# Placing prepared weight tiles at eight byte offsets inside longer rooms, in an order that changes from group to group

## The chip, the cores and the metric

The kernel runs on one core of one Trainium2 chip. The metric is the device time of one execution in microseconds (us). Three runs of the kernel before took 1741.55, 1745.67 and 1746.55 us; their median, 1745.67 us, is the time before.

## The reference: what is computed

One layer of a diffusion backbone over 256 latent and 256 context tokens of width 2048, all in float32: a bidirectional gated linear recurrence (HGRN2, 16 heads of 128) as token mixer, then a gated MLP with a width-3 depthwise convolution. Each sub-layer has a norm before and after it and shift, scale and gate from a linear map of SiLU(c). Only the latent stream is returned. Cut to the core, for the one layer there is:

```python
h_l = modulate(rms_norm(x, norm_mix_pre), sh_ml, sc_ml)          # and h_c from ctx
y_l, _ = hgrn2_mixer(h_l, h_c, hgrn_w_in, lower_bounds, hgrn_o_norm, hgrn_w_out, False)
x = x + gt_ml * rms_norm(y_l, norm_mix_post)
h_l = modulate(rms_norm(x, norm_ffn_pre), sh_fl, sc_fl)
gate, up = jnp.split(h_l @ ffn_w_in, 2, axis=-1)
f_l = (jax.nn.silu(dwconv_centred(gate, conv_w, conv_b)) * up) @ ffn_w_out
return x + gt_fl * rms_norm(f_l, norm_ffn_post)
```

In the mixer `h @ hgrn_w_in` gives q, two forget gates (f, b), v and an output gate g, each of width 2048; the recurrence runs over chunks in both directions, and its normed and gated output goes through `hgrn_w_out`.

## The kernel before, in words

**Three matmuls for one.** Every large product is made by `mm3` (L195 to L199). Each float32 operand is split into a high part, rounded to the matmul's input type, and a low part, the rest. `mm3` adds three products into one bank: high by high (L197), high by low (L198), low by high (L199). In each, `lhsT` is the stationary operand, loaded ahead of the matmul by its own weight load, and `rhs` is the moving operand, streamed through the array.

**The weight stream.** `Stream` (L108) walks all 456 weight tiles of the program in a fixed list: 40 tiles of 2 x 512 columns for the start, 120 of 4 x 256 for the six later head pairs, 32 for `w_out`, 176 for `ffn_w_in` and 88 for `ffn_w_out`. Each holds 1024 float32 values in each of the 128 partitions, 4096 bytes. `load` (L118) brings it into one of four `w_raw` buffers with one DMA on SyncE's queue; `prep` (L125) splits it with `split` (L103): ScalarE casts it to `w_hi` (L105), VectorE writes the rest to `w_lo` (L106). There are three `w_hi` and three `w_lo` buffers (rooms) in `wpool`, and two more of each in `hold` for the last chunk of the mixer's output product. `next` (L144) hands out a tile and keeps two more prepared ahead, so a room is written again as soon as the matmuls of the tile that lay in it are done.

**The stages.** In the start (L347 on) the modulated tokens hTh and hTl come into being two k-tiles at a time, and each pair meets five weight tiles. Then, for each of six head pairs (L869), come the projections f and b (512 columns of hTh and hTl moving, weights stationary), q and g (`proj_ws`, 256 columns moving) and v (`proj_xs`: here the weights are moving, 256 columns, and hTh, hTl stationary). Between their tiles, `step` (L851) lets in pieces of the recurrence (`scan`, float32 matmuls and transposes of 128 columns or fewer) and of the gates' map (`ada_part`). `out_product` (L947) makes the mixer's output product: zh, zl stationary, 512 columns of weights moving. The FFN's first product (L1037 to L1057) has weights stationary and 256 columns of h2h, h2l moving, 4,224 matmuls; its second is `out_product` again with ah, al stationary and 512 columns of weights moving, 1,056 matmuls.

**Places in SBUF.** Tiles lie where their pools put them, one behind the other from the left or, with `side="right"`, from the right end. `spacer` (L57) makes a tile of given length that nobody uses. Four of these concern the change: `spacer(wpool, SHIFT)` (L518, 64 bytes) stands between the `w_raw` and the `w_hi` rooms, `spacer(h2, 256 - SHIFT)` (L933) ahead of h2h and h2l, `spacer(hold[0], SHIFT)` (L940) ahead of the rooms in `hold`; `SHIFT` is 64 (L63). With them, every `w_hi` and `w_lo` begins 64 bytes past a multiple of 128, and so does all that lies behind `wpool` on the left up to h2: keep, st, zpool, sp. hTh, hTl, zh, zl, h2h, h2l, ah and al begin at a multiple of 128. All inner steps (512, 1024 and 2048 bytes) are multiples of 128.

Of the kernel before, what the change touches and what calls it, by code (L numbers as in the profile page):

```python
# [9 lines left out]
F32R = mybir.dt.float32r  # L10
# [7 lines left out]
P = 128  # L18
# [17 lines left out]
def tile_hgrn2_convffn_layer(  # L36
# [13 lines left out]
    wpool = ctx.enter_context(tc.tile_pool(name="wpool", bufs=3))  # L50
# [6 lines left out]
    def spacer(pool, nbytes):  # L57

        pool.tile([P, nbytes // 4], F32, name="spacer", bufs=1)

    SHIFT = 64  # L63
    edge = ctx.enter_context(tc.tile_pool(name="edge", bufs=1, side="right"))
    spacer(edge, 224)

    def bank(pool, name):
        return pool.tile([P, 512], F32, name=name)
# [34 lines left out]
    def split(hi, lo, src):  # L103

        S.copy(out=hi, in_=src)  # L105
        V.tensor_tensor(out=lo, in0=src, in1=hi.bitcast(F32), op=ALU.subtract)  # L106

    class Stream:  # L108


# [14 lines left out]
        def prep(self, pool=wpool):  # L125
            i = len(self.done)
            with tc.high_priority(offset=0 if i < n_start else 400):
                self.load(i + 1)
                _, a, w = self.specs[i]
                hi = pool.tile([P, a, w], F32R, name="w_hi")  # L130
                lo = pool.tile([P, a, w], F32R, name="w_lo")
                if i in self.fine:
                    for j in range(a):
                        split(hi[:, j], lo[:, j], self.raw[i][:, j])
                else:
                    split(hi, lo, self.raw[i])
            self.raw[i] = None
            self.done.append((hi, lo))
# [82 lines left out]
    def rows128(v):  # L221
        return v.rearrange("(r p) -> r p", p=P)
# [26 lines left out]
    def load_tokens(src, tiles):  # L249
        for tt in range(2):  # L250
            t = hpool.tile([P, D], F32, name=f"hTh{len(tiles)}")
            nc.sync.dma_start(out=t, in_=src[tt * P:(tt + 1) * P, :])
            tiles.append(t)
# [11 lines left out]
    def silu_c():  # L265

        tp = bank(ps_mi, "mi")
        PE.transpose(out=tp[:, 0:32], in_=rowsS[0:32, :], identity=ident[0:32, 0:32])
        sgc = st.tile([P, 32], F32, name="sgc")
        S.activation(out=sgc, in_=tp[:, 0:32], func=AF.Sigmoid)  # L270
        V.tensor_tensor(out=cst[:, :, 0:2], in0=tp[:, 0:32].rearrange("p (i k) -> p k i", i=2),
                        in1=sgc.rearrange("p (i k) -> p k i", i=2), op=ALU.mult)
# [6 lines left out]
    def column(dst, src, n):  # L279

        tp = bank(ps_sc, "sc")
        PE.transpose(out=tp[:, 0:n], in_=src[0:n, :], identity=ident[0:n, 0:n])
        V.tensor_copy(out=dst[:, 0:n], in_=tp[:, 0:n])
# [29 lines left out]
    def normed(w):  # L313

        for i in range(2):
            t = xt[2 * w + i]
            ms = small.tile([P, 1], F32, name="ms")
            jk = st.tile([P, D], F32, name="jk")
            S.activation(out=jk, in_=t, func=AF.Square, accum_out=ms)
            r = token_rstd(ms, "rstd")  # L320
            for cs in (slice(0, 256), slice(256, D)):
                V.tensor_scalar(out=t[:, cs], in0=t[:, cs], scalar1=r, scalar2=None, op0=ALU.mult)
# [66 lines left out]
    def ada_load(j2):  # L389
        aws = []  # L390
        for r4 in range(4):
            aw = st.tile([P, 4, 2, 256], F32, name="aw", bufs=4)
            for s in range(2):
                nc.sync.dma_start(
                    out=aw[:, :, s, :],
                    in_=ada_w[r4 * 512:(r4 + 1) * 512, s * D + j2 * 256:s * D + (j2 + 1) * 256].rearrange(
                        "(a p) n -> p a n", p=P))
            aws.append(aw)
        return aws
# [111 lines left out]
    with tc.manual_schedule():  # L511
        nc.sync.dma_start(out=rowsS[0:16], in_=rows128(c[0]))
        nc.sync.dma_start(out=rowsS[16:32], in_=rows128(c_ctx))
        load_tokens(x, xt)
        nc.sync.dma_start(out=rowsB[0:96], in_=rows128(ada_b))
        nc.sync.dma_start(out=rows0[0:16], in_=rows128(n_mix_pre[0]))
        ws.load(1)
        spacer(wpool, SHIFT)  # L518
        aws0 = ada_load(0)
        ws.load(4)  # L520
        V.memset(ones32, 1.0)
        V.memset(one1, 1.0)
        V.memset(eps1, EPS)
        nc.gpsimd.memset(cst, 0.0)
        make_identity(nc, ident)
        silu_c()
        normed(0)
        ws.prep()
        column(colsB, rowsB, 96)
        column(cols0, rows0, 16)  # L530
        strip = bank(ps_o, "o")
        ada_rows(strip, aws0, 0)
        turned(0, 0, KT)
        for r4 in range(1, 4):
            ada_rows(strip, aws0, r4)
        mod0 = ada_mod(0, strip)
        load_tokens(ctx_in, xt)
        for i in range(2):
            q4 = hpool.tile([P, 4, 512], F32R, name=f"hTh{i}")
            for k in range(4):  # L540
                hTh[4 * i + k] = q4[:, k]
        for k in range(2):
            hTl[k] = hpool.tile([P, 512], F32R, name=f"hTl{k}")
        modulated(0, mod0, (0,))
        ws.prep()
        ws.prep()
# [366 lines left out]
    h2h, h2l, xin, hold = [], [], [], []  # L913

    def mixed():

        nonlocal h2
        with tc.high_priority(offset=200):
            split(zh[1], zl[1], z[1])
        for p in (*range(2, NP - 1), 0):  # L920
            split(zh[p], zl[p], z[p])
            for _ in range(MIXSTEP):
                next(mix, None)
            yield
        for _ in mix:
            pass
        split(zh[NP - 1], zl[NP - 1], z[NP - 1])
        yield
        yield
        zp_ctx.close()  # L930
        sp_ctx.close()
        h2 = h_ctx.enter_context(tc.tile_pool(name="h2", bufs=1))
        spacer(h2, 256 - SHIFT)  # L933
        for k in range(KT // 2):
            h2h.append(h2.tile([P, 2, T], F32R, name=f"h2h{k}"))
            h2l.append(h2.tile([P, 2, T], F32R, name=f"h2l{k}"))

        xinp = xin_ctx.enter_context(tc.tile_pool(name="xinp", bufs=1))
        hold.append(xin_ctx.enter_context(tc.tile_pool(name="hold", bufs=MORE)))
        spacer(hold[0], SHIFT)  # L940
        for i in range(4):
            xin.append(xinp.tile([P, D // 2], F32, name=f"xin{i}"))
            nc.sync.dma_start(out=xin[i], in_=x[i // 2 * P:(i // 2 + 1) * P, i % 2 * 1024:(i % 2 + 1) * 1024])

    h2 = None
# [91 lines left out]
    for i in range(NFF):  # L1037
# [6 lines left out]
        for up in range(2):  # L1044
            o = bank(ps_pj, "pj")
            for k4 in range(4):
                hi, lo = ws.next()
# [70 lines left out]
```

## Time and profile before

| what | value |
|---|---|
| runs: lowest, median, highest | 1741.55, 1745.67, 1746.55 us |
| the profiled execution's own time | 1748.88 us |
| its span, first to last instruction | 1747.1 us |
| mean granted TensorE clock | 0.994 |
| instructions | 32106 |
| DMA | 352.57 MB, 202 GB/s in the mean |

The span is what the views below divide up; 1.8 us of the execution lie around it. "PE" is TensorE's matmul side and "PEld" its weight loads, which run beside the matmuls. A matmul's record begins when it begins and ends when its last result is out, so records of matmuls that follow each other closely overlap: how fast they follow is read from the distance of the starts, or from how many stand in a stretch, not from the recorded length. [...]

### The profile page before, as it was taken

Reading aid. Unit: us, or ns where it says so; the run is one execution under the profiler, and the core shown is the slowest. Engines: PE = TensorE matmul, PEld = TensorE weight load, DVE = VectorE, ACT = ScalarE, POOL = GpSimd, SP = SyncE. Lnnn points to the kernel's source line nnn. Section 1 sums busy time; section 2 is a strip of 40 time slices with the busy share of each in tenths; the row PEclk is TensorE's granted clock in tenths of the full one; section 3 lists DMA queues with packets and bytes.
Section 4 is the critical chain, followed back from the end, with each engine's and each line's share of the span. In section 5 each row is a group of like instructions: output and inputs, shape, how many; then the busy total and the mean of one; then the engine's idle time right before and its main releaser. Section 6 shows DMA issues by size and latency. Waiting matters only on the chain.

```text
span 1747.1 us, 32106 instructions
## 1 busy us (share of the span) xinstructions
PE 1689.7 (97%) x13022; PEld 1501.7 (86%) x13022; DVE 1159.0 (66%) x1877; ACT 777.5 (45%) x1197; POOL 3.4 (0%) x13
## 2 busy tenths in 40 slices
PE   6999999999999999999999799999999999999998
PEld 4677888888989889897987598999999999888886
DVE  5777897865649775786566788666666666544444
ACT  4322264454545344343464554444444444443443
POOL 0000000000000000000000000000000000000000
PEclk9999999999999999999999999999999999999999
DMA  9887656653326773776358688666666666655554
GB/s 349 283 290 243 215 171 205 214 164 105 103 84 201 248 241 103 231 226 196 110 176 293 206 262 276 199 194 194 193 194 193 193 194 194 205 199 193 199 191 146
DMA packets 274646, 352.57 MB, mean 202 GB/s; under 512 B 12954, under 2 KB 197675, under 8 KB 273987
## 3 DMA queue, kind: packets, MB, share of 16 engines
q1 hardware_dynamic: 274499, 350.53, 62.4%
q8 instruction: 102, 1.67, 0.4%
q14 instruction: 45, 0.37, 0.1%
HBM read 348.37 MB, written 2.11 MB: 201 GB/s over the span
## 4 chain that ended last, share of the span: by engine, by line
PE 74%; DMA 12%; DVE 9%; issue 3%; ACT 1%; SPq 1%; DVEq 0%; ACTq 0%
PE pj L197 23%; PE pj L198 23%; PE pj L199 23%; DMA ada_w<-in_ada_w_dram 10%; DVE w_lo L106 3%; DVE ada_acc L351 2%; PE o L403 1%; DMA w_raw<-in_hgrn_w_in_dram 1%; DVE k L679 1%; PE sc L719 1%; ACT w_hi L105 1%; PE mi L791 1%; DMA aw<-in_ada_w_dram 1%; DMA hTh<-in_x_dram 0%; DVE QA L679 0%
## 5 line engine op out<-in xcount | busy, mean ns | idle before, releaser
L106 DVE TENSOR_TENSOR w_lo<-w_raw,w_hi 128x1024 fp32r<-128x1024 f32 (+1 forms) x465 | 558.6, 1203 | 364.9 <-ACT w_hi L105 363.8
L105 ACT CAST w_hi<-w_raw 128x1024 fp32r<-128x1024 f32 (+1 forms) x465 | 478.5, 1032 | 704.8 <-PE pj L198 384.7
L199 PE MATMUL pj<-h2h,w_lo 128*128 128x256 f32 x1408 | 389.5, 277 | 4.8 <-DVE w_lo L106 4.7
L197 PE MATMUL pj<-h2h,w_hi 128*128 128x256 f32 x1408 | 389.2, 276 | 0.0
L198 PE MATMUL pj<-h2l,w_hi 128*128 128x256 f32 x1408 | 389.1, 276 | 0.0
L197 PE MATMUL pj<-hTh,w_hi 128*128 128x256 f32 (+1 forms) x1040 | 353.4, 341 | 2.9 <-ACT hTh L105 1.6
L199 PE MATMUL pj<-hTh,w_lo 128*128 128x256 f32 (+1 forms) x1040 | 348.4, 336 | 5.5 <-DVE w_lo L106 5.4
L198 PE MATMUL pj<-hTl,w_hi 128*128 128x256 f32 (+1 forms) x1040 | 348.2, 335 | 0.0
L199 PEld LDWEIGHTS pj<-h2h,w_lo 128*128 128x128 f32 x1408 | 264.3, 188 | 5.9 <-DVE w_lo L106 5.8
L197 PEld LDWEIGHTS pj<-h2h,w_hi 128*128 128x128 f32 x1408 | 264.4, 188 | 0.9 <-issue 0.8
L198 PEld LDWEIGHTS pj<-h2l,w_hi 128*128 128x128 f32 x1408 | 264.4, 188 | 0.2 <-DVE h2l L106 0.2
L351 DVE SCALAR_TENSOR_TENSOR ada_acc<-ada_w,cst,ada_acc 128x512 f32<-128x512 f32 x240 | 179.8, 749 | 82.4 <-DMA ada_w<-in_ada_w_dram 80.2
L197 PEld LDWEIGHTS pj<-hTh,w_hi 128*128 128x128 f32 x1040 | 196.7, 189 | 33.0 <-issue 5.9
L199 PEld LDWEIGHTS pj<-hTh,w_lo 128*128 128x128 f32 x1040 | 196.7, 189 | 28.9 <-DVE w_lo L106 6.3
L198 PEld LDWEIGHTS pj<-hTl,w_hi 128*128 128x128 f32 x1040 | 197.1, 190 | 21.4 <-DVE hTl L106 0.2
L199 PE MATMUL pj<-w_hi,al 128*128 128x512 f32 x352 | 138.7, 394 | 0.0
L198 PE MATMUL pj<-w_lo,ah 128*128 128x512 f32 x352 | 138.0, 392 | 0.0
L197 PE MATMUL pj<-w_hi,ah 128*128 128x512 f32 x352 | 136.6, 388 | 0.0
L197 PE MATMUL pj<-w_hi,hTh 128*128 128x256 f32 (+1 forms) x448 | 134.2, 299 | 1.7 <-DVE q L455 1.5
L198 PE MATMUL pj<-w_lo,hTh 128*128 128x256 f32 (+1 forms) x448 | 132.3, 295 | 0.0
L199 PE MATMUL pj<-w_hi,hTl 128*128 128x256 f32 (+1 forms) x448 | 132.2, 295 | 0.0
L197 PEld LDWEIGHTS pj<-w_hi,hTh 128*128 128x128 f32 x448 | 84.2, 188 | 6.5 <-ACT w_hi L105 1.6
(224 smaller groups left out, 1773.5 us busy)
## 6 DMA issues: line engine op xcount, KB each, us to landing
w_raw<-in_ffn_w_in_dram SPq DMA_DIRECT2D x176, 512.0 KB, 4.0
w_raw<-in_hgrn_w_in_dram SPq DMA_DIRECT2D x160, 512.0 KB, 4.5
ada_w<-in_ada_w_dram SPq DMA_DIRECT2D x256, 256.0 KB, 3.9
w_raw<-in_ffn_w_out_dram SPq DMA_DIRECT2D x88, 512.0 KB, 3.7
aw<-in_ada_w_dram SPq DMA_DIRECT2D x64, 512.0 KB, 8.7
w_raw<-in_hgrn_w_out_dram SPq DMA_DIRECT2D x32, 512.0 KB, 5.7
hTh<-in_x_dram SPq DMA_DIRECT2D x2, 1024.0 KB, 7.0
hTh<-in_ctx_dram SPq DMA_DIRECT2D x2, 1024.0 KB, 12.0
```

What stands on the lines that cost most here:

```text
L105: S.copy(out=hi, in_=src)
L106: V.tensor_tensor(out=lo, in0=src, in1=hi.bitcast(F32), op=ALU.subtract)
L197: PE.matmul(out=o, lhsT=lh, rhs=rh, start=first, stop=False, skip_group_check=True)
L198: PE.matmul(out=o, lhsT=lh, rhs=rl, start=False, stop=False, skip_group_check=True)
L199: PE.matmul(out=o, lhsT=ll, rhs=rh, start=False, stop=last, skip_group_check=True)
L351: V.scalar_tensor_tensor(out=acc, in0=aw, scalar=cst[:, r, 0:1], in1=acc, op0=ALU.mult, op1=ALU.add)
L403: PE.matmul(out=strip[32 * a:32 * (a + 1), :], lhsT=cst[:, r4 * 4 + a, :], rhs=aws[r4][:, a].rearrange("p s n -> p (s n)"), start=(r4 == 0 ...
L679: V.tensor_tensor(out=half(t, i, m), in0=half(t, i, m), in1=half(by, 1 - i, m)[:, :, 0:1].to_broadcast([P, 256 // m, m]), op=ALU.mult)
L719: PE.matmul(out=o[32 * b:32 * b + 32, 32 * i:32 * i + 32], lhsT=flat(lhs[b % 2])[:, s0:s0 + 32], rhs=flat(rhs[b % 2])[:, t0:t0 + 32], star ...
L791: PE.matmul(out=sps[:, cs], lhsT=kT[:, d, h, ct], rhs=v[:, 2 + ct, h * P:(h + 1) * P], start=(ct == 0), stop=(ct == 1))
```

## The change

Each `w_hi` and each `w_lo` now lies inside a room of 4096 + 128 bytes, at an offset that the new function `placed` takes from a table of eight. `i` is the tile's number in the stream; for tile i the table is read at i x m modulo 8, where m goes 1, 3, 5, 7 from one group of eight tiles to the next. A `w_hi` and its `w_lo` have the same offset. The three spacers of `SHIFT` are gone.

```diff
-    SHIFT = 64
...
+    PLACES = [64, 60, 56, 52, 48, 68, 72, 76]
+
+    def placed(pool, a, w, name, i):
+        t = pool.tile([P, a * w + 32], F32R, name=name)
+        o = PLACES[i * (1 + 2 * (i // 8 % 4)) % 8] // 4
+        return t[:, o:o + a * w].rearrange("p (a n) -> p a n", a=a)
...
-                hi = pool.tile([P, a, w], F32R, name="w_hi")
-                lo = pool.tile([P, a, w], F32R, name="w_lo")
+                hi = placed(pool, a, w, "w_hi", i)
+                lo = placed(pool, a, w, "w_lo", i)
...
-        spacer(wpool, SHIFT)
...
-        spacer(h2, 256 - SHIFT)
...
-        spacer(hold[0], SHIFT)
```

In the built program the rooms' starts go from 64 to 0 modulo 128, and so the tiles' starts to 48, 52, 56, 60, 64, 68, 72 or 76 modulo 128. keep, st, zpool and sp go from 64 to 0 modulo 128. hTh, hTl, zh, zl, h2h, h2l, ah and al stay at 0 modulo 128, `w_raw` stays where it was. The instructions, their order on each engine and queue, their shapes and their waits are the same as before.

## Rows read from the trace of the kernel before

**Rows 1.** The page, part 1: busy time, share of the span and instructions.
```profile
span 1747.1 us, 32106 instructions
...
PE 1689.7 (97%) x13022; PEld 1501.7 (86%) x13022; DVE 1159.0 (66%) x1877; ACT 777.5 (45%) x1197; POOL 3.4 (0%) x13
```
**Rows 2.** The page, part 4: the chain that ended last, by engine, by line.
```profile
PE 74%; DMA 12%; DVE 9%; issue 3%; ACT 1%; SPq 1%; DVEq 0%; ACTq 0%
PE pj L197 23%; PE pj L198 23%; PE pj L199 23%; DMA ada_w<-in_ada_w_dram 10%; DVE w_lo L106 3%; DVE ada_acc L351 2%; PE o L403 1%; DMA w_raw<-in_hgrn_w_in_dram 1%; DVE k L679 1%; PE sc L719 1%; ACT w_hi L105 1%; PE mi L791 1%; DMA aw<-in_ada_w_dram 1%; DMA hTh<-in_x_dram 0%; DVE QA L679 0%
```
**Rows 3.** Waits of TensorE for prepared weights: us in total, times, longest.
```profile
PE pj L199 <- DVE w_lo L106: 10.1, 6, 4.2
...
PE pj L198 <- DVE w_lo L106: 4.9, 4, 2.3
...
PE pj L197 <- ACT w_hi L105: 3.0, 3, 1.7
```
**Rows 4.** Two stretches of the FFN: length, PE busy (matmuls), clock, DMA share, GB/s.
```profile
1240.00:1490.00 250.00, 250.00 (x2208) 1.00 0.63 193
1500.00:1735.00 235.00, 235.00 (x1028) 1.00 0.57 189
```
**Rows 5.** Timeline, projections f and b, 512 columns: start us, length us, what.
```profile
234.51 0.39 PE L197 MATMUL pj<-hTh,w_hi 128*128 128x512 f32 x1
...
256.68 0.39 PE L199 MATMUL pj<-hTh,w_lo 128*128 128x512 f32 x1
```
**Rows 6.** Timeline, a v projection, its second matmul and its last.
```profile
316.33 0.28 PE L198 MATMUL pj<-w_lo,hTh 128*128 128x256 f32 x1
...
327.41 0.28 PE L199 MATMUL pj<-w_hi,hTl 128*128 128x256 f32 x1
```
**Rows 7.** Timeline, a later v projection, first and last.
```profile
641.71 0.28 PE L197 MATMUL pj<-w_hi,hTh 128*128 128x256 f32 x1
...
652.48 0.28 PE L199 MATMUL pj<-w_hi,hTl 128*128 128x256 f32 x1
```
**Rows 8.** Timeline, from a q projection over four transposes into a v projection.
```profile
531.88 0.28 PE L197 MATMUL pj<-hTh,w_hi 128*128 128x256 f32 x1
...
533.47 0.28 PE L199 MATMUL pj<-hTh,w_lo 128*128 128x256 f32 x1
533.58 0.60 PE L831 MATMUL mi<-ident,tmp 128*128 128x128 f32 x4
...
534.14 0.28 PE L198 MATMUL pj<-w_lo,hTh 128*128 128x256 f32 x1
...
534.96 0.28 PE L199 MATMUL pj<-w_hi,hTl 128*128 128x256 f32 x1
```
**Rows 9.** Groups of matmuls in 641.7 to 652.3 us: busy us, mean ns.
```profile
L198 PE MATMUL pj<-w_lo,hTh 128*128 128x256 f32 x31 | 8.6, 276 | 0.0
```
**Rows 10.** Groups of matmuls in 317 to 327 us.
```profile
L198 PE MATMUL pj<-w_lo,hTh 128*128 128x256 f32 x29 | 8.1, 280 | 0.0
```
**Rows 11.** The page, part 5: the two casts; busy us, mean ns, idle before, releaser.
```profile
L106 DVE TENSOR_TENSOR w_lo<-w_raw,w_hi 128x1024 fp32r<-128x1024 f32 (+1 forms) x465 | 558.6, 1203 | 364.9 <-ACT w_hi L105 363.8
L105 ACT CAST w_hi<-w_raw 128x1024 fp32r<-128x1024 f32 (+1 forms) x465 | 478.5, 1032 | 704.8 <-PE pj L198 384.7
```
**Rows 12.** Groups of matmuls over the whole span, by shape: busy us, mean ns.
```profile
L198 PE MATMUL pj<-h2l,w_hi 128*128 128x256 f32 x1408 | 389.1, 276 | 0.0
...
L198 PE MATMUL pj<-hTl,w_hi 128*128 128x512 f32 x496 | 196.2, 396 | 0.0
...
L199 PE MATMUL pj<-w_hi,al 128*128 128x512 f32 x352 | 138.7, 394 | 0.0
...
L198 PE MATMUL pj<-w_lo,hTh 128*128 128x256 f32 x384 | 107.0, 279 | 0.0
L199 PE MATMUL pj<-w_hi,hTl 128*128 128x256 f32 x384 | 106.9, 278 | 0.0
...
L791 PE MATMUL mi<-v,kT 128*128 128x128 f32 x128 | 19.7, 277 | 0.1
```

## Prediction

> **What bounds the kernel now.** I read the page's busy times first: TensorE is busy for 1689.7 of 1747.1 us, VectorE for 1159.0 and ScalarE for 777.5 [rows 1]. So a cast that takes longer costs nothing as long as its tile still arrives in time. The chain of waits says the same: TensorE alone holds 74% of it, and the three lines of mm3 (L197, L198, L199) some 69% [rows 2]. TensorE's own waits are short: all waits of L197 to L199 for prepared weights together are 10.1 + 4.9 + 3.0 = 18.0 us [rows 3]. What is left is the pace at which one matmul follows another while nothing makes TensorE wait, and that is read from the start times, since the recorded lengths overlap.
>
> [...] The v projection shows both paces with one and the same code: 94 starts in 327.41 - 316.33 = 11.08 us, 117.9 ns each, in one group [rows 6], and 95 in 652.48 - 641.71 = 10.77 us, 113.4 ns each, in a later one [rows 7]. [...] Which one holds is inherited: from 531.88 to 533.47 us 14 starts are 114 ns apart; then four transposes come in between, and from 534.14 us on 7 starts are 117 ns apart [rows 8]. The recorded lengths tell the pace too: for L198 276 ns in the group at 113.4 and 280 in the group at 117.9 [rows 9, 10].
>
> **The change part by part.** No instruction is added, removed or moved: on all five queues the order, the waits and the shapes stay as they were, and every DMA still writes w_raw at the place it had. Only places in SBUF change. Before, w_hi and w_lo begin 64 bytes past a multiple of 128 and the activations (hTh, hTl, zh, h2h, ah) at a multiple of 128, so the two operands of mm3 stand 64 bytes apart modulo 128 (but for the 12 matmuls that take z0 from ada_acc). After, the rooms begin at a multiple of 128 and the tile in them at 48 to 76 bytes; the activations keep a multiple of 128. The distance is then one of eight values, another one for each weight tile, that is, after every 48 matmuls or fewer. The change does do what it says: both tiles of a pair get the same place.
>
> *The casts.* L105 and L106 write and read at the new places, 1032 and 1203 ns in the mean [rows 11]. I cost this at nothing. The cover is the time in which ScalarE waits for TensorE to free a room, of its 704.8 us of idle time before L105 384.7 end with an L198 that frees a room [rows 11]; in the FFN a tile feeds 24 matmuls of 113.3 ns = 2.7 us, more than twice the longer cast. If all casts grew by a tenth, VectorE would have 56 us more work and TensorE's 18.0 us of waits would grow by a few us at most.
>
> *The scan and the other pools* (keep, zpool, sp, st) move from 64 to 0 modulo 128, operands together, so their distances stay; only the transposes against ident change theirs. Were all 128 records of L791 [rows 12], the longest group there, to change by one step of 4.5 ns, that is 0.6 us; I take 0.
>
> *The pace of mm3.* This is the whole sum. No row shows a distance other than 64 that isn't a multiple of 64, so the price is bounded from both sides. The nearest rows are the two paces, 4.5 ns apart.
> - 512 columns of hTh: 1,488 matmuls (3 x 496), all at the longer pace by their mean lengths of 396 ns, and the group at 233.4 is one of them [rows 5, 12]. If all took the shorter pace, 1,488 x 4.5 = 6.7 us would go. The trace shows the shorter one at this width only with other operands [rows 4], so I take half: -3.3 us.
> - v projection: 3 x 384 = 1,152. Their mean lengths, 279 and 278 ns for L198 and L199 [rows 12], lie between 276 and 280, some six to seven tenths of the way, so about 0.7 x 1,152 = 806 run at the longer pace. With a new distance for each tile the pace is not inherited for long; I take all of them: 806 x 4.5 = -3.6 us.
> - FFN: 3 x 1,408 and 3 x 352 matmuls are at the shorter pace already [rows 4, 12]; I take 0.
> Sum: -7.0 us. The profiled execution took 1748.88 us, 1.8 outside its span and 3.2 above the median of the runs; against itself the sum gives 1741.9, against the median of 1745.67 it gives **1738.7**.
>
> The ends of this cost. Below: all of both terms (6.7 + 3.6) and one more step of 4.5 ns in the FFN's 4,224 matmuls, 19.0 us, are 29.3 us: 1716.4. [...] Above: see the second rival.
>
> [...]
>
> **The rivals.**
> 1. *Nothing changes: 1745.7.* Which pace holds is decided by what came before, not by places: [rows 6 to 8] show both paces at the same distance of 64, and the first product of the FFN keeps a mean length of 276 ns over all its groups [rows 12]. Against it: the 512-column stream is never seen at its shorter pace, which a mere accident of timing would not explain. Chance 0.30, with gains and losses that cancel within 5.2 us counted here. [...]
> 2. *The FFN loses its pace: 1762.* It holds the better pace with all 5,280 matmuls at one fixed distance. If a new distance for each tile makes it draw a pace anew, as the interruption at 533.58 us does for the v projection [rows 8], and it draws the longer one as often as v does now, seven tenths: 0.7 x (4,224 + 1,056) x 4.5 = 16.6 us more, with nothing gained elsewhere. It beats the forecast's 7.0 us from a share of 0.3 on, and shows as slower by itself from 0.22 on (5.2 of 23.8 us). Chance 0.17.
> 3. [...] Chance 0.11.
> [...]
>
> **How the numbers follow.** About 0.3% of this kernel, 5.2 us, is what a measurement can tell from no change. Forecast (faster by over 5.2 us): 0.42; its own range is 1716 to 1740. Rival 1: 0.30. Rivals 2 and 3: 0.17 + 0.11 = 0.28, all slower. Range: from the lower end of the cost, 1716, to the second rival's 1762, which leaves out the casts becoming late and a loss of pace in more than seven tenths of the FFN, about 2 in 10 with what lies below 1716.
>
> **What would show it.** Right: the group of 512 columns of hTh falls from a mean length of 396 ns towards 392, and the v projection's to 276, while the FFN's first product keeps 2,208 matmuls in 250 us, and the rest of the page stays. Wrong: the FFN's mean length above 277 ns or fewer than 2,190 starts in 250 us (rival 2); lengths up by 1 to 2 ns in all groups alike (rival 3); the same two paces in the same groups (rival 1); waits of L197 to L199 for w_hi or w_lo above 18.0 us would mean that the casts were not free; and an FFN under 112 ns per matmul would mean that the gain has a source that the two paces don't show.

## The result, and the profile after

The changed kernel took 1762.91 us (median of 4 runs, 1761.57 to 1764.15), the kernel before 1746.03 us in the same comparison (4 runs, 1741.55 to 1746.55): the ratio is 1.0107, 95% interval [1.0085, 1.0129]. It is slower by 1.1%, where 1738.7 us had been forecast; the range ended 0.9 us below it. The profiled execution took 1761.57 us.

The page of the changed kernel, parts 1, 4 and 5. The lines of mm3 are now L203 (high by high), L204 (high by low) and L205 (low by high), those of `split` L103 and L104.

```profile
span 1759.8 us, 32106 instructions
...
PE 1713.0 (97%) x13022; PEld 1524.2 (87%) x13022; DVE 1159.1 (66%) x1877; ACT 777.6 (44%) x1197; POOL 3.4 (0%) x13
...
PE 76%; DMA 11%; DVE 8%; issue 3%; ACT 2%; SPq 0%; DVEq 0%; ACTq 0%
...
L104 DVE TENSOR_TENSOR w_lo<-w_raw,w_hi 128x1024 fp32r<-128x1024 f32 (+1 forms) x465 | 558.9, 1203 | 384.9 <-ACT w_hi L103 384.0
L103 ACT CAST w_hi<-w_raw 128x1024 fp32r<-128x1024 f32 (+1 forms) x465 | 478.6, 1032 | 721.8 <-PE pj L204 394.7
```

Against [rows 1, 11]: the instructions are the same, VectorE and ScalarE are as busy as before, and a cast takes 1032 and 1203 ns, to the ns as before. TensorE alone is busy 23 us longer, with the same 13022 matmuls. The groups of matmuls over the whole span, by shape, tell where:

```profile
L203 PE MATMUL pj<-h2h,w_hi 128*128 128x256 f32 x1408 | 394.8, 280 | 1.4 <-ACT h2h L103 1.4
L205 PE MATMUL pj<-h2h,w_lo 128*128 128x256 f32 x1408 | 394.4, 280 | 3.3 <-DVE w_lo L104 3.3
L204 PE MATMUL pj<-h2l,w_hi 128*128 128x256 f32 x1408 | 394.0, 280 | 0.1
...
L204 PE MATMUL pj<-hTl,w_hi 128*128 128x512 f32 x496 | 196.0, 395 | 0.0
...
L205 PE MATMUL pj<-w_hi,al 128*128 128x512 f32 x352 | 138.9, 395 | 0.0
...
L204 PE MATMUL pj<-w_lo,hTh 128*128 128x256 f32 x384 | 108.7, 283 | 0.0
...
L796 PE MATMUL mi<-v,kT 128*128 128x128 f32 x128 | 19.7, 276 | 0.1
```

The FFN's first product went from 276 to 280 ns, v from 279 to 283, while the 512-column projections of hTl fell by 1 ns only, and the scan's longest group stayed [rows 12]. The stretch that [rows 4] show, 1240 to 1490 us, at the same granted clock of 1.00:

```profile
1240.00:1490.00 250.00, 250.00 (x2134) 1.00 0.60 187
```

2,134 matmuls instead of 2,208, so one per 117.3 ns instead of 113.3. In this kernel, timelines of the first product can be read tile by tile: 24 matmuls meet each weight tile. These are the first matmuls of eleven tiles in a row, whose places are 76, 64, 52, 72, 60, 48, 76, 56, 68, 64 and 68:

```profile
1301.58 0.28 PE L203 MATMUL pj<-h2h,w_hi 128*128 128x256 f32 x1
...
1304.30 0.28 PE L203 MATMUL pj<-h2h,w_hi 128*128 128x256 f32 x1
...
1307.02 0.28 PE L203 MATMUL pj<-h2h,w_hi 128*128 128x256 f32 x1
...
1309.74 0.28 PE L203 MATMUL pj<-h2h,w_hi 128*128 128x256 f32 x1
...
1312.61 0.28 PE L203 MATMUL pj<-h2h,w_hi 128*128 128x256 f32 x1
...
1315.45 0.28 PE L203 MATMUL pj<-h2h,w_hi 128*128 128x256 f32 x1
...
1318.29 0.28 PE L203 MATMUL pj<-h2h,w_hi 128*128 128x256 f32 x1
...
1321.05 0.28 PE L203 MATMUL pj<-h2h,w_hi 128*128 128x256 f32 x1
...
1323.89 0.28 PE L203 MATMUL pj<-h2h,w_hi 128*128 128x256 f32 x1
...
1326.74 0.28 PE L203 MATMUL pj<-h2h,w_hi 128*128 128x256 f32 x1
...
1329.47 0.28 PE L203 MATMUL pj<-h2h,w_hi 128*128 128x256 f32 x1
```

From row to row: 76, 64 and 52 take 2.72 us each (113.3 ns a matmul); then 72 takes 2.87, 60 and 48 2.84, 76 now 2.76, 56 2.84, 68 2.85; 64 takes 2.73 again. The pace follows the place, but not in every tile: over the whole product 18 of the 22 tiles at 64 stay under 114.2 ns in the mean, 12 of 22 at 52 and 9 of 22 at 76. Two whole tiles at 64 run at 118.3 and 118.8 ns.

For the sums below, "pace" is the mean distance between the starts of two matmuls of mm3 that follow each other directly, without distances over 133 ns (256 columns) or 267 ns (512), which are stalls.

| stream (distances) | before, ns | after, ns | cost, us |
|---|---|---|---|
| FFN, first product (4,221) | 113.36 | 117.30 | +16.6 |
| q, g and other 256 columns of hTh (1,605) | 114.22 | 117.68 | +5.6 |
| f, b, 512 columns of hTh (1,448) | 233.28 | 232.27 | -1.5 |
| v, weights moving (1,130) | 116.44 | 119.12 | +3.0 |
| FFN, second product (1,055) | 228.89 | 232.49 | +3.8 |
| mixer's output and v at the start (379 + 190) | 229.22, 230.74 | 232.64, 233.28 | +1.8 |

Together +29.3 us. The stalls in these streams fell from 38.3 to 27.6 us, since the casts kept their 1032 and 1203 ns while a weight tile of the first product lasts 24 x 117.3 ns instead of 24 x 113.4; TensorE's waits in mm3 for prepared weights alone went from 18.0 us [rows 3] to 12.1:

```profile
PE pj L205 <- DVE w_lo L104: 6.0, 5, 1.9
PE pj L203 <- ACT w_hi L103: 3.4, 3, 1.5
PE pj L204 <- DVE w_lo L104: 2.7, 2, 1.5
```

29.3 - 10.7 = 18.6 us stand against a difference of the medians of 16.9, and of the two spans of 12.7, where the profiled execution before lay 2.9 us above its median. By the starts of the stages in these two profiles the FFN's two products take 17.6 us longer (489.4 to 503.1 us and 241.8 to 245.7), while the FFN begins 4.8 us earlier (1003.6 against 1008.4 us); what is gained ahead of the FFN is not assigned to anything.

### The profile page after: what moved, and what is told of

It is laid out like the page before. It is cut to its first block, busy times and chain, and to the rows that moved or that the text cites. A ratio compares the mean times of both kernels' runs of the same rounds, so it can differ in the third digit from the quotient of the medians.

```text
span 1759.8 us, 32106 instructions
## 1 busy us (share of the span) xinstructions
PE 1713.0 (97%) x13022; PEld 1524.2 (87%) x13022; DVE 1159.1 (66%) x1877; ACT 777.6 (44%) x1197; POOL 3.4 (0%) x13
## 4 chain that ended last, share of the span: by engine, by line
PE 76%; DMA 11%; DVE 8%; issue 3%; ACT 2%; SPq 0%; DVEq 0%; ACTq 0%
PE pj L203 24%; PE pj L205 23%; PE pj L204 23%; DMA ada_w<-in_ada_w_dram 10%; DVE ada_acc L357 2%; DVE w_lo L104 2%; PE o L409 2%; ACT w_hi L103 1%; PE sc L724 1%; PE mi L796 1%; DVE k L684 1%; DMA w_raw<-in_hgrn_w_in_dram 1%; DMA aw<-in_ada_w_dram 0%; PE pj L337 0%; PE mi L712 0%
## 5 line engine op out<-in xcount | busy, mean ns | idle before, releaser
L104 DVE TENSOR_TENSOR w_lo<-w_raw,w_hi 128x1024 fp32r<-128x1024 f32 (+1 forms) x465 | 558.9, 1203 | 384.9 <-ACT w_hi L103 384.0
L103 ACT CAST w_hi<-w_raw 128x1024 fp32r<-128x1024 f32 (+1 forms) x465 | 478.6, 1032 | 721.8 <-PE pj L204 394.7
L205 PE MATMUL pj<-h2h,w_lo 128*128 128x256 f32 x1408 | 394.4, 280 | 3.3 <-DVE w_lo L104 3.3
L203 PE MATMUL pj<-h2h,w_hi 128*128 128x256 f32 x1408 | 394.8, 280 | 1.4 <-ACT h2h L103 1.4
L204 PE MATMUL pj<-h2l,w_hi 128*128 128x256 f32 x1408 | 394.0, 280 | 0.1
L203 PE MATMUL pj<-hTh,w_hi 128*128 128x256 f32 (+1 forms) x1040 | 354.4, 341 | 2.5 <-ACT hTh L103 1.6
L205 PE MATMUL pj<-hTh,w_lo 128*128 128x256 f32 (+1 forms) x1040 | 348.5, 336 | 2.8 <-DVE w_lo L104 2.7
L204 PE MATMUL pj<-hTl,w_hi 128*128 128x256 f32 (+1 forms) x1040 | 348.3, 335 | 0.0
L205 PEld LDWEIGHTS pj<-h2h,w_lo 128*128 128x128 f32 x1408 | 265.4, 188 | 4.0 <-DVE w_lo L104 3.7
L203 PEld LDWEIGHTS pj<-h2h,w_hi 128*128 128x128 f32 x1408 | 264.7, 188 | 2.4 <-ACT h2h L103 1.5
L204 PEld LDWEIGHTS pj<-h2l,w_hi 128*128 128x128 f32 x1408 | 265.4, 188 | 0.3 <-DVE h2l L104 0.3
L203 PEld LDWEIGHTS pj<-hTh,w_hi 128*128 128x128 f32 x1040 | 195.8, 189 | 32.2 <-issue 5.9
L205 PEld LDWEIGHTS pj<-hTh,w_lo 128*128 128x128 f32 x1040 | 195.8, 189 | 25.8 <-DVE w_lo L104 3.6
L204 PEld LDWEIGHTS pj<-hTl,w_hi 128*128 128x128 f32 x1040 | 196.3, 189 | 21.1 <-DVE hTl L104 0.2
L205 PE MATMUL pj<-w_hi,al 128*128 128x512 f32 x352 | 138.9, 395 | 0.0
L203 PE MATMUL pj<-w_hi,ah 128*128 128x512 f32 x352 | 138.9, 395 | 0.0
L204 PE MATMUL pj<-w_lo,ah 128*128 128x512 f32 x352 | 138.6, 394 | 0.0
L203 PE MATMUL pj<-w_hi,hTh 128*128 128x256 f32 (+1 forms) x448 | 136.4, 305 | 1.7 <-ACT w_hi L103 1.0
L205 PE MATMUL pj<-w_hi,hTl 128*128 128x256 f32 (+1 forms) x448 | 134.1, 299 | 0.0
L204 PE MATMUL pj<-w_lo,hTh 128*128 128x256 f32 (+1 forms) x448 | 134.0, 299 | 0.0
L203 PEld LDWEIGHTS pj<-w_hi,hTh 128*128 128x128 f32 x448 | 85.4, 191 | 6.7 <-DVE stage L459 1.8
```

The costliest lines, as they stand in the source:

```text
L203: PE.matmul(out=o, lhsT=lh, rhs=rh, start=first, stop=False, skip_group_check=True)
L204: PE.matmul(out=o, lhsT=lh, rhs=rl, start=False, stop=False, skip_group_check=True)
L205: PE.matmul(out=o, lhsT=ll, rhs=rh, start=False, stop=last, skip_group_check=True)
```

## The experiments

### Is it the change of place, the place, or the rooms?

Three theories. P: each place has its own pace. C: a change of place from tile to tile breaks a pace that is otherwise kept (the forecast's second rival). R: the longer rooms, and the pools that moved 64 bytes, do it whatever the place. Three runs, each with one line of the change altered.

```diff
-    PLACES = [64, 60, 56, 52, 48, 68, 72, 76]
+    PLACES = [64] * 8                               # e1_all64
+    PLACES = [56] * 8                               # e2_fixed56
+    PLACES = [64, 52, 76, 64, 52, 76, 64, 52]       # e3_three
```

> The change's longer rooms and moved pools, but every tile at 64 bytes. Theories: P (place: the distance of weights and activations modulo 128 sets the pace; 64 keeps 113.3 ns, most of the other seven cost about 5 ns more per matmul), C (change: any change of distance makes a stream draw its pace anew, a constant one doesn't), R (rooms: the longer rooms or the moved pools cost the time, not the offsets). P and C: 1743 to 1749 us, about 2,208 matmuls in 250 us of the FFN's first product. R: 1758 us or more.

> Every tile at 56 bytes, never changed. P: the FFN's first product at 118.5 ns as its tiles at 56 show in the changed kernel, 4,224 x 5.2 = 22 us, and its second product 1,056 x 2.8 = 3 us: 1766 to 1775 us. C: no change of distance, so 1743 to 1749 us. R: 1763 us as the changed kernel.

> Places 64, 52 and 76 only, in the change's own order. P: these three hold 113.3 ns once they have it, so 1743 to 1752 us. C: the distance changes as often as in the change, so 1758 us or more. R: 1763 us.

| | us | ratio to before | FFN, first product: pace, ns |
|---|---|---|---|
| all at 64 | 1741.91 | 0.9994 [0.9977, 1.0010] | 113.38 |
| all at 56 | 1766.97 | 1.0132 [1.0095, 1.0169] | 118.36 |
| 64, 52, 76 in turn | 1746.27 | 1.0006 [0.9987, 1.0025] | 113.54 |

R falls with the first run, C with the two others: one fixed place costs more than the change did, and three places that change with each tile cost nothing that the interval shows. A stretch of the first product in the run at 64 (it ends there at 1487 us), then 1240 to 1490 us of the run at 56, then of the one with three places:

```profile
1240.00:1485.00 245.00, 245.00 (x2164) 1.00 0.63 194
```

```profile
1240.00:1490.00 250.00, 250.00 (x2111) 1.00 0.60 185
```

```profile
1240.00:1490.00 250.00, 250.00 (x2209) 1.00 0.63 194
```

### Which stage carries the loss?

```diff
-        o = PLACES[i * (1 + 2 * (i // 8 % 4)) % 8] // 4
+        o = (64 if 192 <= i < 368 else PLACES[i * (1 + 2 * (i // 8 % 4)) % 8]) // 4   # e9
+        o = (PLACES[i * (1 + 2 * (i // 8 % 4)) % 8] if 192 <= i < 368 else 64) // 4   # e10
```

Tiles 192 to 367 are those of the FFN's first product.

> The change's order of eight places everywhere, but every weight tile of the FFN's first product at 64. Theory F (the FFN's first product, at its places other than 52, 64 and 76, carries the loss; the same places cost the mixer and the FFN's second product less): FFN's first product at 113.4 ns per matmul as before, its stage near 489 us, the mixer's 256-column streams at 117 to 119 ns and the second product at 232 as in the change; the whole 1747 to 1753 us. Rival (each stage loses in proportion to its matmuls): half of the change's 17 us stays, 1754 us or more. Rival (the loss needs the dither only somewhere, the pace is inherited): FFN at 117 ns although its tiles lie at 64.

> The change's order of eight places in the FFN's first product alone, 64 for all other weight tiles. Theory F: FFN's first product at 117.3 ns, its stage near 503 us, all else as with all tiles at 64; the whole 1756 to 1761 us. Rival (each stage in proportion): 1753 us or less.

The change everywhere but there: 1746.78 us against 1741.71, 1.0026 [1.0008, 1.0043]. The change there alone: 1755.3 us, 1.0079 [1.0058, 1.0099]. The two add up to 1.05%, the change's own 1.07%. The first product has 113.45 ns in one and 117.31 in the other: the pace is not handed on from an earlier stage. Theory F is right; both times lie just under the ranges expected for it, 1747 to 1753 and 1756 to 1761 us. The stretch of 1240 to 1490 us of the one, then of the other:

```profile
1240.00:1490.00 250.00, 250.00 (x2209) 1.00 0.64 194
```

```profile
1240.00:1490.00 250.00, 250.00 (x2134) 1.00 0.61 186
```

### The map of places

Each place for eight tiles on end, in steps of 4 bytes: first rising from 0 to 84, then falling from 124 to 40, so that all 32 places within 128 bytes are seen and those from 40 to 84 entered from both sides.

```diff
+    FFN_AT = [0, 4, 8, 12, 16, 20, 24, 28, 32, 36, 40, 44, 48, 52, 56, 60, 64, 68, 72, 76, 80, 84]
...
+        if 192 <= i < 368:
+            return FFN_AT[(i - 192) // 8]
...
-        o = PLACES[i * (1 + 2 * (i // 8 % 4)) % 8] // 4
+        o = place(i) // 4
```

> A map: in the FFN's first product group g of eight tiles lies at 4 x g bytes (0 to 84), in the second product eight tiles each at 0, 8, ... 80, in the mixer one place per head pair (0, 16, 32, 52, 76, 96), else 64. P: the pace of a group follows its place: 113.3 ns at 52, 64, 76 and at some others still unknown, 117 to 120 at 48, 56, 60, 68, 72. C: within a group, after its first tile, every place settles at 113.3 or 117.8 ns without regard to the place. R: all groups alike.

> The second map, in falling order: group g of the FFN's first product at 124 - 4 x g bytes (124 to 40), the second product's tiles at 124, 116 ... 44, the mixer's head pairs at 112, 84, 64, 48, 36, 20. P: the places 40 to 84 show the pace that the first map gave them though they now follow another neighbour: 113.4 ns at 52, 64, 76 and 117 to 120 ns elsewhere; 88 to 124 are new. If the pace were handed on from group to group instead, the groups after 76 and 64 would keep 113.4.

Stretches of 20 us of the rising map, at places 48, 52, 56, 60, 64, 68, 72 and 76:

```profile
1284.00:1304.00 20.00, 20.00 (x170) 1.00 0.60 184
1306.00:1326.00 20.00, 20.00 (x179) 1.00 0.64 192
1328.00:1348.00 20.00, 20.00 (x171) 1.00 0.60 186
1351.00:1371.00 20.00, 20.00 (x171) 1.00 0.60 185
1373.00:1393.00 20.00, 20.00 (x179) 1.00 0.62 187
1395.00:1415.00 20.00, 20.00 (x172) 1.00 0.61 186
1418.00:1438.00 20.00, 20.00 (x171) 1.00 0.60 186
1440.00:1460.00 20.00, 20.00 (x179) 1.00 0.63 189
```

179 against 170 to 172. By the starts, 52, 64 and 76 run at 113.4 ns, and the means of all 29 others over their eight tiles lie between 116.9 (place 12) and 120.5 (place 20). In the falling map 64 has 113.4 and 76 settles at 113.6, but 52, entered from 56, stays at 118.2: 52 and 76 can keep the fast pace but do not always restore it. The FFN's second product, where the weights move, ran at 228.7 (place 124) to 237.2 ns (place 84) in these two runs, from one execution each: there the place counts too, with another order. The whole kernels took 1761.78 and 1768.24 us, of which nothing follows, since several stages were moved at once.

The high and the low tile in different places, eight tiles for each pair:

```diff
+    PAIRS = [(64, 64), (64, 56), (56, 64), (64, 60), (60, 64), (64, 72), (72, 64), (64, 76), ...]
...
+            return PAIRS[(i - 192) // 8][name == "w_lo"]
```

> A map in which w_hi and w_lo lie at different places, one pair per group of eight tiles in the FFN's first product: (64,64), (64,56), (56,64), (64,60), (60,64), (64,72), (72,64), (64,76), (76,64), (64,52), (52,64), (64,0), (0,64), (64,32), (32,64), (64,96), (96,64), (52,76), (76,52), (52,52), (76,76), (56,56). Two thirds of the weight loads read w_hi, one third w_lo. If each load's own distance counts: 113.4 ns where both are of 52, 64, 76; about 115 where only w_lo is off, about 117 where only w_hi is. If one disturbed load in three upsets the whole stream: 117 to 119 wherever either is off.

(64, 56) runs at 117.5 ns, (56, 64) at 117.7, (64, 60) and (60, 64) at 118.2 and 118.6, (64, 76), (76, 64) and (64, 52) at 113.3. In (64, 56) only one of three weight loads is at a bad place, and the mean is still 117.5 ns; two matmuls at 113.3 and one at 118.3, the pace of (56, 56), would make 115.0. But (52, 64) ran at 117.8 and (52, 76) at 119.5 although each of their places alone can be fast; that is not explained. The other mixed pairs, with 72, 0, 32 or 96 beside 64, and (76, 52), ran at 116.4 to 118.2; (52, 52) and (76, 76) at 113.4, (56, 56) at 118.3. The whole took 1755.99 us.

The kernel before with 128 bytes between its high and its low rooms, so that every `w_lo` begins at 192 modulo 256 (the spacer ahead of h2 is 128 bytes shorter, which keeps h2 where it was):

```diff
                 hi = pool.tile([P, a, w], F32R, name="w_hi")
+                if i == 0:
+                    pool.tile([P, 32], F32, name="between", bufs=1)
                 lo = pool.tile([P, a, w], F32R, name="w_lo")
```

> The kernel before with 128 bytes between the w_hi and the w_lo rooms, so that modulo 256 w_hi stays at 64 and w_lo goes to 192; modulo 128 nothing moves. If 128 bytes are the whole period: the kernel before, 1741 to 1748 us, and 233.3 and 228.9 ns for the two 512-column streams. If the period is longer: the 512-column streams move as they did with all tiles at 64 in the longer rooms (231.6 and 230.8 ns), and the time by 2 us or less.

1742.43 us, 0.9996 [0.9968, 1.0023]. FFN's first product keeps 113.4 ns; but f and b fall from 233.3 to 231.8, and where the weights move the pace rises: FFN's second product from 228.9 to 230.4, v from 116.4 to 117.7. The run with all tiles at 64 has the same paces (231.6, 230.8, 117.6). That is a side of the change that the prediction did not see: with rooms of 4096 + 128 bytes, a `w_lo` lies an odd multiple of 128 from its `w_hi`, before it was a multiple of 256.

### Place, or distance to the other operand?

If only the distance modulo 128 between weights and activations counts (theory D), then moving both by 120 bytes from where 64 was must keep the pace. The weights are all at 56 and h2h, h2l at 120:

```diff
-            h2h.append(h2.tile([P, 2, T], F32R, name=f"h2h{k}"))
-            h2l.append(h2.tile([P, 2, T], F32R, name=f"h2l{k}"))
+            for got, name in ((h2h, f"h2h{k}"), (h2l, f"h2l{k}")):
+                room = h2.tile([P, 2 * T + 32], F32R, name=name)
+                got.append(room[:, 30:30 + 2 * T].rearrange("p (a t) -> p a t", a=2))
```

> Every weight tile at 56 bytes as in the fixed one, and h2h and h2l at 120 bytes modulo 128, so that the FFN's first product has both operands off the multiples of 16 but 64 apart again. If the distance sets the pace: that product falls from 118.4 to 113.4 ns per matmul, 4,224 x 5.0 = 21 us less than the fixed one: 1744 to 1749 us. If a place off the multiples of 16 costs by itself: it stays at 118 ns and the time at 1765 us or more.

1772.6 us, 1.017 [1.0122, 1.0219], and 120.28 ns: worse than any kernel here. I took that as the end of theory D. The next four runs used the same longer rooms: h2 at 64 (30 becomes 16), at 12 (30 becomes 3), then by quarters of the k-tiles, `o = [0, 32, 64, 96][k // 2] // 4`, and `[0, 0, 16, 80]`, with the weights' places changing every eight tiles.

> h2h and h2l begin 64 bytes past a multiple of 128 instead of 0; the FFN's weight tiles change place every eight tiles: 64, 0, 52, 0, 76, 0, 116, 0, 12, 0, 56, ... Theory D (only the distance modulo 128 counts, good at 52, 64, 76): 0, 116 and 12 run at 113.4, and 64, 52 and 76 at 117 to 120. Theory W (only the weights' place counts): 64, 52 and 76 run at 113.4 and 0, 116, 12 at 117 to 120. Theory B (both places count, the weights' at 52, 64, 76 and the activations' at 0): nothing runs at 113.4. One look, read from the starts of the matmuls in each place; the total says nothing.

> h2h and h2l begin 12 bytes past a multiple of 128; the FFN's weight tiles change place every eight tiles: 64, 76, 0, 12, 52, 64, 68, 4, 88, 80, ... Theory D: 76, 64 and 88 run at 113.4, 52 does not. Theory W: 52, 64 and 76 do, 88 does not. Theory B: none, since the activations' place is not at the start of a 64-byte half; by the run with both moved (activations at 120) this is the likeliest. One look.

> h2h and h2l lie in rooms 128 bytes longer, as in the runs that moved them, but the k-tiles 0 to 3 begin at 0, 4 to 7 at 32, 8 to 11 at 64 and 12 to 15 at 96 modulo 128; every weight tile meets one of the four. The FFN's weight tiles stand at 64 in every other group or so and at 96, 0, 32, 16, 80, 48, 112, 52, 76, 116, 12, 20, 44 between. Theory B (the weights' place and the activations' place both count): with weights at 64 the first quarter runs at 113.4 ns and the others at 117 to 119. Rival (the longer rooms of h2h and h2l did it in the runs that moved them, not their place): the first quarter runs at 117 to 119 too. Read also whether any of the 56 pairs runs below 113.3, which would be a place better than that of the kernel before. One look.

> As the run by quarters, with k-tiles 0 to 7 at 0, 8 to 11 at 16 and 12 to 15 at 80 modulo 128. Theory B: with weights at 64 the first half of each eight k-tile pairs runs at 113.4 ns, the rest at 117 to 119. Rival (the longer rooms): all at 117 to 119. One look.

No place of the weights ran at 113.4 ns with h2 at 64 (117.2 and more) or at 12 (116.4 and more); the totals were 1759.6 and 1749.97 us. The last two runs then took theory B away as well: with the weights at 64 and the activations at 0, the very pair of the kernel before, the first quarter ran at 118.9 to 121.2 ns and the first half at 118.8 to 121.3 (whole kernels 1761.35 and 1756.29 us). So the rooms themselves spoilt it: at 2048 + 128 bytes each, an h2l lies an odd multiple of 128 behind its h2h, in all five runs. (Both ranges are of means over the tiles of one place that meet the same k-tiles.) Two more runs separate this distance of the parts from the place of both: one moves all of h2 by a spacer and leaves the rooms at 2048; the other has rooms of 2048 + 256 and moves h2l alone.

```diff
         h2 = h_ctx.enter_context(tc.tile_pool(name="h2", bufs=1))
+        spacer(h2, 64)                                                        # e15
...
+                room = h2.tile([P, 2 * T + 64], F32R, name=name)              # e16
+                o = (got is h2l) * [0, 0, 64, 128][k // 2] // 4
+                got.append(room[:, o:o + 2 * T].rearrange("p (a t) -> p a t", a=2))
```

> A spacer of 64 bytes ahead of h2h and h2l, whose rooms keep their length: all of them begin 64 bytes past a multiple of 256, and a high and its low part stay a multiple of 256 apart, as in the kernel before. The FFN's weight tiles change place every eight tiles: 64, 0, 52, 0, 76, 0, 116, 0, 12, ..., as in the run with h2 at 64 in longer rooms. Theory D (the distance modulo 128 between weights and activations sets the pace, good at 52, 64 and 76; in the four runs with longer rooms a second condition was broken, that the high and the low part of the activations lie a multiple of 256 apart): 0 runs at 113.4 ns, 116 and 12 too when entered from 0, and 64, 52, 76, 56 at 117 to 120; the whole near 1750 us. Theory W (only the weights' place): 64, 52 and 76 at 113.4. Theory B (both places for themselves): nothing at 113.4. One look.

> All weights at 64. The rooms of h2h and h2l are 256 bytes longer; each h2h begins at a multiple of 256, and h2l a multiple of 256 behind it for k-tiles 0 to 7, 64 more for 8 to 11, 128 more for 12 to 15. Theory D with its second condition: k-tiles 0 to 7 at 113.4 ns, 12 to 15 (and 8 to 11) at 117 to 121, the FFN's stage some 10 us longer. Rival (longer rooms of the activations cost the pace whatever the distance of the parts): all at 117 or more. Rival (the parts' distance is nothing): 113.4 for 0 to 7 and 12 to 15. One look.

Stretches of the run with the spacer; the weights are at 116, 0, 12 and 0 in the first (84 us), at 56 in the second, at 0, 112 and 0 in the others:

```profile
1143.00:1227.00 84.00, 84.00 (x744) 1.00 0.63 194
1232.00:1251.00 19.00, 19.00 (x163) 1.00 0.57 175
1299.00:1318.00 19.00, 19.00 (x169) 1.00 0.61 188
1456.00:1476.00 20.00, 20.00 (x170) 1.00 0.60 183
1480.00:1498.00 18.00, 18.00 (x161) 1.00 0.60 186
```

The first stretch of the run with h2 at 64 in the longer rooms, with the same weights' places:

```profile
1143.00:1227.00 84.00, 84.00 (x710) 1.00 0.62 187
```

With h2 at 64 and its parts a multiple of 256 apart, the weights at 0, 116 and 12, which are 64, 52 and 76 bytes away modulo 128, settle at 113.3 to 113.6 ns (one block of 0, entered from 76, at 114.1, its first two tiles at 118.8), and 64, 52, 76 and 56 run at 116.9 to 118.8. So the good place moved with the activations: theory D, and not the weights' place. That holds for a shift of 64 bytes; no other shift was tried with the parts a multiple of 256 apart. In the run on the low part these are the first matmuls of five tiles in a row, k-tiles 0 to 3, 4 to 7, 8 to 11, 12 to 15 and 0 to 3 again:

```profile
1305.95 0.28 PE L204 MATMUL pj<-h2h,w_hi 128*128 128x256 f32 x1
...
1308.67 0.28 PE L204 MATMUL pj<-h2h,w_hi 128*128 128x256 f32 x1
...
1311.39 0.28 PE L204 MATMUL pj<-h2h,w_hi 128*128 128x256 f32 x1
...
1314.22 0.28 PE L204 MATMUL pj<-h2h,w_hi 128*128 128x256 f32 x1
...
1317.04 0.28 PE L204 MATMUL pj<-h2h,w_hi 128*128 128x256 f32 x1
```

2.72 and 2.72 us with the parts a multiple of 256 apart, 2.83 with 64 more, 2.82 with 128 more. Over the product the paces are 113.3 for k-tiles 4 to 7, settled 113.8 for 0 to 3 (a few matmuls to recover), 117.5 to 118.3 for 8 to 11 and 119.1 to 121.3 for 12 to 15 (means by quarters of a tile; whole tiles of 12 to 15 run at 117.7, as the one shown, or up to 121.8). The step of 64 also puts `h2l` at a bad distance from the weights, 0 modulo 128, so it is no test of the parts' distance by itself; the step of 128 leaves that distance at 64 and is one. So there are two conditions, and both have to hold. The wholes took 1752.17 and 1748.79 us.

### Both conditions met in longer rooms

With longer rooms for h2h and h2l the FFN had begun at 988 to 996 us, with the short ones in the run with the spacer and in the one with all tiles at 64 at 1002 and 999, so the last two runs ask two things: whether the pace holds when every part meets both conditions, and whether a kernel better than both comes of it.

```diff
+            for got, name in ((h2h, f"h2h{k}"), (h2l, f"h2l{k}")):
+                room = h2.tile([P, 2 * T + 64], F32R, name=name)
+                got.append(room[:, :2 * T].rearrange("p (a t) -> p a t", a=2))
```

Once on the kernel with all tiles at 64, once on the kernel before.

> All weights at 64 in rooms of 4096 + 128 bytes, h2h and h2l in rooms 256 bytes longer, all at 0 modulo 256. Theory D with its second condition: both distances are good, so the FFN's first product runs at 113.4 ns in every quarter, against 116.4 in the run on the low part; 4,221 x 3.0 ns = 13 us less than that run's one look of 1749 us: 1733 to 1740 us, if its mixer, which ended some 10 us earlier than with the shorter rooms, does so again; 1741 to 1745 if that is given back as stalls at the FFN's start. Rival (longer rooms of the activations cost the pace by themselves): 1748 us or more.

> The kernel before with h2h and h2l in rooms 256 bytes longer, all at 0 modulo 256 as before. Theory D: FFN's first product at 113.4 ns, its second at 228.9, v at 116.4, f and b at 233.3 as before; 1733 to 1745 us by the same argument. Rival (longer rooms cost the pace): 1760 us or more.

1742.19 us, 0.9996 [0.9971, 1.0021], and 1743.35 us, 1.0021 [0.9986, 1.0057]. The pace holds in the main, at 113.45 and 113.77 ns, so longer rooms as such do not take it away. The mixer did end earlier (the FFN begins at 992 us in both profiles, against 1008 in the one before and 999 with all tiles at 64), but the stalls in the first product grew from 7.0 to 13 us, and against the runs of before no gain is left.

The mean of 113.77 hides something. In the last run, with both distances good in every matmul, parts of the first product run at the slow pace after a wait for a weight tile. Four stretches without a wait:

```profile
1029.00:1039.00 10.00, 10.00 (x87) 1.00 0.92 301
1095.00:1103.00 8.00, 8.00 (x70) 1.00 0.91 297
1105.00:1113.00 8.00, 8.00 (x71) 1.00 0.90 293
1123.00:1143.00 20.00, 20.00 (x179) 1.00 0.72 220
```

The first three run at 117.8 ns by the starts, for up to 95 matmuls on end and in part through further interruptions; the last is at 113.3. So the two distances make the fast pace possible, and which of the two paces a stream has at them can still depend on what interrupted it, as in the v projections of the kernel before [rows 6, 7]. Why it does is open. That DMA was busy in the slow stretches is not enough, since the kernel before kept the fast pace in this one:

```profile
1029.00:1039.00 10.00, 10.00 (x90) 1.00 0.87 280
```

No kernel of this study is measurably faster than the one before.

## Why the prediction was wrong

**The bound** was read rightly: TensorE's pace, not the casts, set the time. The casts kept their lengths to the ns and the scan's longest group its own within 1 ns, so both cost nothing that can be seen, as costed.

**The step that failed** is the FFN's term, "are at the shorter pace already; I take 0". It costs 4,221 x 3.94 ns = 16.6 us in the first product and 3.8 in the second. No reason was given for the nothing. For v the prediction argued: "With a new distance for each tile the pace is not inherited for long", and counted that as a gain; the same argument, put to the FFN's streams, which had the fast pace to lose, stood only under the second rival. Behind it stands the sentence that the pace "is inherited", read from the transposes [rows 8] and the v projections [rows 6, 7], which show two paces at one distance. The runs show that this is half of it: the fast pace of the first product is there only at two distances of operands, of which the change broke the first in five places out of eight. Inheritance is real too, at 52 and 76, and at 64 in v (113.4 and 117.9 ns), in two of 22 tiles of the changed kernel (118.3 and 118.8) and in the last run (117.8); but at a bad distance no fast pace was seen to be inherited: of the changed kernel's 110 tiles at 48, 56, 60, 68 and 72 none has a mean below 117.7 ns.

**A stream is missing from the sum.** The 1,632 matmuls with 256 columns of hTh (q, g and a part of the start) had no term. They went from 114.22 to 117.68 ns and cost 5.6 us, the second largest item. The 512 columns of the mixer's output product, also without a term, lost some 1.3 us.

**512 columns of hTh, -3.3 us:** -1.5 (233.28 to 232.27). All tiles at 64 in the longer rooms give 231.6, and the 128 bytes between high and low rooms alone give 231.8, so this small gain came from the rooms, and the new places gave 0.7 ns of it back. That this stream stood at the longer of two paces no run bears out: it is seen at 230.4 to 233.8 ns, and never at the 228.9 of the second product. **v, -3.6 us:** +3.0; it lost by the rooms (116.4 to 117.6) and again by the places (119.1).

**The second rival** named the place and the size: 16.6 us and 1762 us. Its mechanism was half wrong. A change of place does not draw the pace anew: 56 for all tiles costs more than the change (1766.97 against 1762.91 us), and 64, 52, 76 in turn cost nothing that the interval shows (1.0006 [0.9987, 1.0025]). That its 0.7 x 5,280 x 4.5 ns agrees with the measured first product is partly chance: the pace there rose by 3.94 ns over all tiles, and the second product's 3.8 us and the mixer's come on top, less the stalls that got shorter. Its chance of 0.17 was too low: [rows 4] had 2,208 matmuls at one steady pace, and a change that moves operands by up to 16 bytes had nothing to gain there, only to lose.

**The first rival** (nothing changes) falls: the same instructions take 113.4 or 118.4 ns by the place of the stationary operand (all tiles at 64, all at 56).

**The third rival** (chance 0.11) rested on a cost of starts that are no multiple of 16 bytes, and no run shows one. In the first product 52 and 76 are no multiples of 16 and run at 113.4 ns, while 0, 16, 32, 48, 80, 96 and 112 are, and run at 117.7 or more.

**The range** ended at the second rival's price with the FFN's share set at seven tenths. Its lower end counts a step of 4.5 ns below the FFN's pace, and no run shows such a pace: the lowest mean of a tile in the first product is 113.3 ns in the profile before and in the one after. The signals that the prediction listed did name the outcome: a first product above 277 ns (280) and under 2,190 starts in 250 us (2,134).

## What to carry to other kernels

Where TensorE is the bound and a weight load runs beside each matmul, read whether the places of the operands in SBUF set the pace. Here, in the FFN's first product, 113.4 ns a matmul came only where the stationary operand lay 64 bytes (52 and 76 held too) from the moving one modulo 128, against 116.9 to 120.5 at the 29 other places, and where the two moving operands that alternate lay a multiple of 256 apart, against 117.7 and more with 128 bytes more between them. A longer room, a spacer or a new pool in front can change either distance, so after any change of layout read the pace from the distance of starts, stage by stage, against the trace before. A steady pace at its best value is a cover that a change of places can take away, as it did here for 16.6 us, and it belongs into the sum with a price.

## What the runs showed of the hardware

- The first product has a sharp optimum: in the two maps, of 32 places only three keep 113.4 ns, and the others, in the mean over eight tiles, cost 3.5 to 7.1 ns a matmul, at a granted clock of 1.00 in every stretch shown.
- In most tiles 64 restores the fast pace (18 of 22 tiles of the changed kernel are under 114.2 ns in the mean), in the maps of places within a tile, but not always: the run with the spacer has two tiles, the changed kernel two, and the last run stretches of up to 95 matmuls at 117.8 to 118.8 ns at that distance. 52 and 76 hold the fast pace when entered fast (in the changed kernel, after a 64 at 113.3 ns, 113.4 and 113.5); 52, entered from 56, held the slow one (118.2 ns) for eight tiles.
- The two parts of the moving operand count: with the weights 64 from both, 128 bytes off a multiple of 256 cost 4 to 8 ns a matmul in the mean of a tile (117.7 to 121.8 against 113.3). In the first product, where the weights are stationary, 128 bytes between `w_hi` and `w_lo` change nothing (113.4 ns). Where the weights move, they cost: 228.9 to 230.4 ns in the FFN's second product, 116.4 to 117.7 in v.
- The 512-column streams are not settled: f and b get faster by those 128 bytes (233.3 to 231.8), and at place 20 in the falling map ran at 230.4. By that, 1,488 x 2.9 ns = 4.3 us would be an estimate of what a better place for f and b alone is worth; it was not tried.
- What in the chip makes these distances good stays open: the runs show where the pace holds, not why.
